# Ten gate/up pairs of a feed-forward layer: three of eight k steps by Strassen's seven products

## The chip, the cores and the metric

The kernel runs on one core of a Trainium2 chip. The metric is the device time of one execution in microseconds (us). TensorE is called PE here, its weight load PEld, VectorE DVE, ScalarE ACT, GpSimd POOL, and the queue that issues the weight transfers SP.

## The reference, cut

One layer of a decoder trunk on 256 tokens. The change touches the feed-forward part, the last four lines.

```python
h   = RMSNorm(x)                                   # x: (1, 256, 2048) float32
z   = h @ w_in                                     # one combined projection, 2048 x 19472
A   = GLA(h)                                       # chunked gated linear attention, 4 heads
Bm  = DilatedAttn(h)                               # 3 groups of 8 heads, joined by their denominators
y   = sigmoid(ga) * (A @ w_branch_gla) + sigmoid(gb) * (Bm @ w_branch_dil)
x   = x + y @ w_out
hf = _rmsnorm(x, ffn_norm[l])
gu = hf @ w_ffn_in[l]                              # 2048 x 11264
gate, up = gu[..., :D_FF], gu[..., D_FF:]          # D_FF = 5632
x = x + (jax.nn.silu(gate) * up) @ w_ffn_out[l]    # 5632 x 2048
out = _rmsnorm(x, final_norm)
```

## The kernel before

**Tiling.** All large products run over weights streamed once from HBM. A `Job` is one block of 512 output columns (or fewer) over `nkt` tiles of 128 rows (k tiles). Its weights come in units of four k tiles (1 MB, `dma`, line 172) into one of three `raw` buffers, and each unit is used in two subs of two k tiles, 128x1024 elements. `split` (line 184) makes two tiles of a sub: ACT copies it, rounded to fp32r, into `wh`, and DVE subtracts that from the raw tile into `wl`. There are five buffers of each (`LA` = 4 subs of lookahead). `mains` (line 241) then issues, for each k tile and each half of the tokens (128 rows), three matmuls into one PSUM bank: hi x wh, hi x wl and lo x wh, where hi and lo are the split activations, held stationary, and 512 weight columns move. A sub is 12 such matmuls, a gate or up job 8 subs or 96 matmuls, a gate/up pair 192.

**Order.** The program is written out in one order for all engines. For each sub the main loop emits, in this order: the split of the sub `LA` later, the evacuation of the job that ended just before (`pending.evac`), a hook of the job (`pre`), one step of a queue of small generators (`advance`), the matmuls of the sub, one more `advance`. Each engine works through its own part of this order; the tile framework puts in the waits.

**The feed-forward part.** Eleven pairs (`pair(p)`): a gate job, evacuated by two ACT instructions (Silu, `evac_fgate`), then an up job, evacuated by two DVE instructions (line 801, `evac_fup`). The product of 256 tokens x 512 columns is then turned by eight transposes into `psa` (`turn_block`, line 703) and split again by ACT and DVE (line 105). After pairs 4 and 8, and at the end, `down` multiplies the last four (at the end three) blocks by w_ffn_out in four jobs of 512 columns, each added into `x1` by DVE (line 810).

**PSUM** has eight banks of 128x512: four `acc`, one `psa` of two banks, two `psb`. A job in the feed-forward part takes two banks, `fpair` goes round acc, psb and acc.

**End.** The last job runs its token halves apart (lines 241 and 938), so that the final norm of the first half lies beside the matmuls of the second. In it, the sixth sub's split goes into `h` blocks.

Of the kernel before, what the change touches and what calls it, by code (L numbers as in the profile page):

```python
# [16 lines left out]
P = 128  # L17
D = 2048
S = 256
# [27 lines left out]
class Job:  # L47
# [2 lines left out]

    def __init__(self, kind, w, row0, nkt, col0, ncols, ktu, acts, evac, pre=None, pairs=None):
        self.pairs = pairs
        self.kind, self.w, self.row0, self.nkt = kind, w, row0, nkt
        self.col0, self.ncols, self.ktu = col0, ncols, ktu
        self.acts, self.evac, self.pre = acts, evac, pre or {}
# [3 lines left out]
def trunk_layer(ctx: ExitStack, tc: tile.TileContext, x, attn_norm, w_in, w_gk_up, b_gk, gla_norm,  # L61
# [18 lines left out]
    def ps_a():  # L80
        return psum.tile([P, 1024], F32, name="psa", tag="psa", bufs=1)
# [62 lines left out]
    epst = const.tile([P, 1], F32, name="epst")  # L144
    nc.vector.memset(epst, EPS)

    def add(job):
        jobs.append(job)
        job.subs = []
        job.units = []  # L150
        u1 = 0
# [12 lines left out]
        for i, s in enumerate(job.subs):  # L164
            s["last"] = i == len(job.subs) - 1

    def dma(unit):
        job = unit["job"]
        k, n = unit["k"], job.ncols
        unit["raw"] = ring.tile([P, 2048], F32, name="raw", tag="raw", bufs=NRAW)  # L170
        r0 = job.row0 + unit["k0"] * P
        nc.sync.dma_start(unit["raw"][:, :k * n].rearrange("p (a n) -> p a n", a=k),
                          job.w[r0:r0 + k * P, job.col0:job.col0 + n].rearrange("(a p) n -> p a n", p=P))

    def split(sub):
        n, k = sub["job"].ncols, sub["k"]
        src = sub["unit"]["raw"][:, sub["s0"] * n:(sub["s0"] + k) * n]
        if sub["job"] is jobs[-1] and sub["idx"] > LA:
            wh, wl = (block("h", 2 * (sub["idx"] - LA) + i, F32R) for i in range(2))
        else:  # L180
            wh = ring.tile([P, 1024], F32R, name="wh", tag="wh", bufs=LA + 1)
            wl = ring.tile([P, 1024], F32R, name="wl", tag="wl", bufs=LA + 1)
        act(wh[:, :k * n], src, AF.Copy)
        nc.vector.tensor_sub(wl[:, :k * n], src, wh[:, :k * n].bitcast(F32))  # L184
        sub["w"] = [t[:, :k * n].rearrange("p (a n) -> p a n", a=k) for t in (wh, wl)]

    def mains(sub, only=None, part=None):
        job = sub["job"]
        n = job.ncols
        wh, wl = sub["w"]  # L190
        if not hasattr(job, "acc"):
# [66 lines left out]
    def idle(n):  # L258

        for _ in range(2 * n + 1):  # L260
            yield
# [432 lines left out]
            act(z, z, AF.Sigmoid)  # L694
        return go

    def turn_block(src, hl):

        yield from idle(1)
        pt = ps_a()  # L700
        for j in range(4):
            for a in range(2):
                nc.tensor.transpose(pt[:, j * S + a * P:j * S + a * P + P], src[:, a, j * P:(j + 1) * P], ident)  # L703
        yield
        split_act(hl, pt.rearrange("p (j t) -> p j t", j=4))

    def evac_branch(key, i, last):
        def go(job):
# [42 lines left out]
    def reload_x():  # L751
        dctx.close()
        env["fp"] = ctx.enter_context(tc.tile_pool(name="ftmp", bufs=1))
        x1.extend(load_x("o", 4))
        for i in range(2):
            t = block("o", i)
            env["fg", i] = t
            nc.gpsimd.dma_start(t, bass.AP(tensor=final_norm.tensor, offset=final_norm.offset + i * 1024,
                                           ap=[[0, P], [1, 1024]]))

    def ffn_norm_chunk(c):
        yield from idle(1)
        hl = hl_block("h", 2 * c)
        x1T.append(hl)
        yield from to_blocks(x1[c], cols[:, 4 * c:4 * c + 4], hl, range(4),
                             quarters(ps_a()))
        if c == 3:
            tot = const.tile([P, 2], F32, name="tot1")
            nc.vector.tensor_reduce(tot, ss1, AX.X, ALU.add)
            env["rstd2"] = col_rstd("ffn", tot, D)  # L770

    def evac_out(c):
        def go(job):
            for a in range(2):
                nc.vector.tensor_add(x1[c][:, a], job.acc[a], x1[c][:, a])
                junk = env["fp"].tile([P, 512], F32, name="junk", tag="junk")
# [12 lines left out]
    def evac_fgate(p):  # L789
# [4 lines left out]
                act(z[:, a], job.acc[a], AF.Silu, scale=env["rstd2"][:, a:a + 1])  # L794
        return go

    def evac_fup(p):
        def go(job):
            z = env["sg"]
            for a in range(2):  # L800
                nc.vector.scalar_tensor_tensor(z[:, a], job.acc[a], env["rstd2"][:, a:a + 1], z[:, a],
                                               op0=ALU.mult, op1=ALU.mult)
            aT[p] = hl_block("z", (2 * p + 2) % 10)
            push("A", turn_block(z, aT[p]))
        return go

    def evac_down(c, last):
        def go(job):
            for a in range(2):
                nc.vector.tensor_add(x1[c][:, a], job.acc[a], x1[c][:, a])  # L810
                if last:
                    junk = env["fp"].tile([P, 512], F32, name="junk", tag="junk")
# [7 lines left out]
    def pair(p):  # L820
        for col, ev in ((512 * p, evac_fgate(p)), (FF + 512 * p, evac_fup(p))):
            first = (p, col) == (0, 0)
            add(Job("T", w_ffn_in, 0, KT, col, 512, 4, x1_acts, ev,
                    {5: lambda: drain("X")} if first else None, pairs=fpair()))

    def down(p0, n, last):
        acts = lambda ki, p0=p0: (aT[p0 + ki // 4], ki % 4)
        for c in range(4):
            pre = {2 * (n - 1): lambda: drain("A")} if c == 0 else None
            add(Job("T", w_ffn_out, p0 * 512, 4 * n, 512 * c, 512, 4, acts, evac_down(c, last), pre, pairs=fpair()))  # L830

# [84 lines left out]
    for i in range(done, len(subs) - len(jobs[-1].subs)):  # L916
        sub = subs[i]
        next_split()
        if i == 9:
            push("S", input_rstd())  # L920
        if pending and (pending is not jobs[0] or i >= 12):
            pending.evac(pending)
            pending = None
        hook = sub["job"].pre.get(sub["idx"])
        if hook:
            hook()
        advance()
        mains(sub)
        advance()
        if sub["last"]:  # L930
            pending = sub["job"]
# [4 lines left out]
    def add_tokens(src, a, q):  # L936
        w = slice(q * S, q * S + S)
        nc.vector.tensor_add(x1[3][:, a, w], src, x1[3][:, a, w])
        junk = env["fp"].tile([P, 512], F32, name="junk", tag="junk")
# [74 lines left out]
```

## Time and profile before

| | us |
|---|---|
| median of 3 runs | 1885.34 (1884.31 to 1885.46) |
| the profiled execution's own time | 1884.67 |
| its span, first to last instruction | 1882.9 |
| PE busy | 1868.8, 9324 instructions |
| DVE busy | 1025.3 |
| ACT busy | 861.2 |
| DMA engines, mean share of the span | some 5 tenths |

A matmul's recorded duration (386 ns in the mean) overlaps the next one's, so the pace of PE is read from a stretch divided by its count, not from the mean. DVE and ACT durations overlap their neighbours by less than 0.1 us. Between the span and the execution's own time lie 1.8 us.

### The profile page before, as it was taken

The numbers are of one execution on the slowest core, as the hardware profiler recorded it, in microseconds if no ns is written. First come the engines' busy times: TensorE is split into PE (matmuls) and PEld (weight loads), VectorE is DVE, ScalarE is ACT, GpSimd is POOL, SyncE is SP. The second block draws the span as 40 slices with busy tenths as digits, with TensorE's granted clock in tenths as the row PEclk, the third lists the DMA queues.
The fourth block names the chain that finished last, engine by engine and source line by source line (L and its number), as shares of the span: only waits on it lengthen the run. The fifth ranks groups of instructions, "written<-read, shape, count | busy, mean of one in ns | idle before, by whom it ended". The sixth has DMA issues, their size and how long they took to land.

```text
span 1882.9 us, 22862 instructions
## 1 busy us (share of the span) xinstructions
PE 1868.8 (99%) x9324; PEld 1589.8 (84%) x9324; DVE 1025.3 (54%) x1146; ACT 861.2 (46%) x1071; POOL 22.2 (1%) x35
## 2 busy tenths in 40 slices
PE   8999999999999999999999999999999999999998
PEld 8988988888888888888888888888888888888886
DVE  6446646745675466555554555444455454454454
ACT  6446545544454454544444455444443444434443
POOL 0000000000000000000000000000000000000001
PEclk9999999999999999999999999999999999999999
DMA  7554455456555565465657655555555555555553
GB/s 251 205 198 158 166 191 166 165 185 194 171 174 179 201 194 173 164 216 195 213 188 240 230 180 198 184 198 182 197 181 199 194 186 185 195 191 190 197 181 114
DMA packets 207299, 356.32 MB, mean 189 GB/s; under 512 B 6124, under 2 KB 66600, under 8 KB 207193
## 3 DMA queue, kind: packets, MB, share of 16 engines
q1 hardware_dynamic: 202192, 346.18, 54.2%
q0 software_dynamic: 1728, 5.51, 1.4%
q10 hardware_dynamic: 3272, 3.16, 0.6%
q8 instruction: 73, 1.20, 0.2%
q14 instruction: 34, 0.27, 0.0%
HBM read 352.70 MB, written 2.13 MB: 188 GB/s over the span
## 4 chain that ended last, share of the span: by engine, by line
PE 99%; DVE 0%; DMA 0%; ACT 0%; SPq 0%; issue 0%; DVEq 0%; ACTq 0%
PE acc L241 67%; PE psb L241 12%; PE acc L217 9%; PE acc L220 5%; PE psa L703 1%; PE psa L557 1%; PE psb L602 0%; PE psa L478 0%; PE psb L460 0%; PE psb L567 0%; PE psb L604 0%; PE psa L578 0%; DMA o<-in_x_dram 0%; PE psa L308 0%; PE psa L241 0%; PE psb L405 0%
## 5 line engine op out<-in xcount | busy, mean ns | idle before, releaser
L184 DVE TENSOR_TENSOR wl<-raw,wh 128x1024 fp32r<-128x1024 f32 (+2 forms) x655 | 794.3, 1216 | 784.6 <-ACT wh L121 783.1
L121 ACT ACTIVATE wh<-raw 128x1024 fp32r<-128x1024 f32 (+2 forms) x655 | 685.4, 1049 | 862.1 <-PE acc L241 642.2
L241 PE MATMUL acc<-wh,h 128*128 128x512 f32 (+2 forms) x2496 | 768.5, 386 | 0.0
L241 PEld LDWEIGHTS acc<-wh,h 128*128 128x128 f32 x2496 | 467.3, 188 | 91.3 <-issue 1.3
L241 PE MATMUL acc<-wl,h 128*128 128x512 f32 (+2 forms) x1248 | 480.0, 385 | 0.0
L241 PEld LDWEIGHTS acc<-wl,h 128*128 128x128 f32 x1248 | 235.1, 188 | 44.2 <-DVE wl L184 0.3
L241 PE MATMUL acc<-wh,z 128*128 128x512 f32 (+1 forms) x648 | 199.2, 386 | 0.0
L217 PE MATMUL acc<-h,wh 128*128 128x512 f32 x768 | 196.4, 397 | 0.0
L217 PEld LDWEIGHTS acc<-h,wh 128*128 128x128 f32 x768 | 138.5, 189 | 26.9 <-issue 0.7
L241 PEld LDWEIGHTS acc<-wh,z 128*128 128x128 f32 x648 | 121.1, 188 | 24.3
L241 PE MATMUL acc<-wl,z 128*128 128x512 f32 (+1 forms) x324 | 125.0, 386 | 0.0
L241 PE MATMUL psb<-wh,h 128*128 128x512 f32 x384 | 119.9, 390 | 0.0
L220 PEld LDWEIGHTS acc<-h,wl 128*128 128x128 f32 x768 | 104.6, 190 | 7.8
L220 PE MATMUL acc<-h,wl 128*128 128x256 f32 x768 | 106.9, 282 | 0.0
L241 PE MATMUL psb<-wh,z 128*128 128x512 f32 x304 | 94.9, 390 | 0.0
L241 PE MATMUL acc<-h,wh 128*128 128x256 f32 x512 | 92.5, 283 | 0.0
L241 PEld LDWEIGHTS psb<-wh,h 128*128 128x128 f32 x384 | 72.1, 188 | 14.9
L241 PEld LDWEIGHTS acc<-h,wh 128*128 128x128 f32 x512 | 80.0, 192 | 0.2
L241 PE MATMUL acc<-wh,o 128*128 128x512 f32 x256 | 79.5, 389 | 0.0
L241 PE MATMUL psb<-wl,h 128*128 128x512 f32 x192 | 74.7, 389 | 0.0
L241 PE MATMUL acc<-h,wl 128*128 128x256 f32 x256 | 72.4, 283 | 0.0
L241 PEld LDWEIGHTS acc<-wl,z 128*128 128x128 f32 x324 | 60.9, 188 | 12.1
(202 smaller groups left out, 1151.5 us busy)
## 6 DMA issues: line engine op xcount, KB each, us to landing
raw<-in_w_in_dram SPq DMA_DIRECT2D x144, 1024.0 KB, 4.7
raw<-in_w_ffn_in_dram SPq DMA_DIRECT2D x88, 1024.0 KB, 4.8
raw<-in_w_ffn_out_dram SPq DMA_DIRECT2D x44, 1024.0 KB, 5.0
raw<-in_w_branch_gla_dram SPq DMA_DIRECT2D x16, 1024.0 KB, 5.0
raw<-in_w_out_dram SPq DMA_DIRECT2D x16, 1024.0 KB, 5.0
raw<-in_w_branch_dil_dram SPq DMA_DIRECT2D x8, 1024.0 KB, 5.0
raw<-in_w_in_dram SPq DMA_DIRECT2D x8, 692.0 KB, 3.9
z<-in_b_gate_dram POOLq DMA_DIRECT2D x8, 512.0 KB, 8.0
```

What stands on the lines that cost most here:

```text
L121: nc.scalar.activation(o, i, func, **kw)
L184: nc.vector.tensor_sub(wl[:, :k * n], src, wh[:, :k * n].bitcast(F32))
L217: nc.tensor.matmul(job.acc[j], wh[:, kk, c], hl.both(aj), start=ki == 0, stop=ki == job.nkt - 1, skip_group_check=True)
L220: nc.tensor.matmul(job.acc[j][:, 0:S], wl[:, kk, c], hl.hi(aj), start=False, stop=ki == job.nkt - 1, skip_group_check=True)
L241: nc.tensor.matmul(dst, st, mv, start=first and i == 0 and j % per_bank == 0, stop=last and i == 2, skip_group_check=True)
L557: nc.tensor.matmul(p1[:, g * 256:(g + 1) * 256], qk[g][:, 0, 128:256], qk[g][:, 1], start=g != 1, stop=True, skip_group_check=True)
L703: nc.tensor.transpose(pt[:, j * S + a * P:j * S + a * P + P], src[:, a, j * P:(j + 1) * P], ident)
```

## The change

The product of two k tiles, both token halves and the gate and up columns is a 2x2 by 2x2 block product: A11, A12 (first token half, k tiles 0 and 1), A21, A22 (second half); B11, B12 (k tile 0, gate and up), B21, B22 (k tile 1). In pairs 1 to 10 gate and up become one job of kind "S" with eight steps of two k tiles. Five steps (0, 1, 3, 5, 7) are direct, with eight block products of three matmuls; three (`FAST` = 2, 4, 6) take seven, by Strassen's algorithm in Winograd's form, with sums of activation blocks (`x1_forms`, made once, used by all ten pairs) and sums of weight blocks (`sums`, made by DVE for each step). Pair 0 stays as it was.

- A direct step has two subs (b1, b2: one k tile, gate and up, 12 matmuls each). A Strassen step has four: b11 (512 wide, 3 matmuls), b2, t13 and t24 (1024 wide, 6 matmuls each). A job has 22 subs where a pair had 16.
- The 1 MB of a step (two k tiles, gate and up columns) comes in two transfers of 512 KB; before, the 1 MB of four k tiles of one job came in one.
- Eight PSUM banks are summed up in a job: p2, p3, p4, p8 by all steps, p1, p5, p6, p7 by the Strassen steps alone. The second four are read by `evac_step1` while step 7 runs, the first four by `evac_step2` after the job. `turn` says which four are in `acc`; it alternates between pairs that follow each other.
- From the first "S" job the lookahead is five subs, with one more buffer pair (blocks z8, z9) as every sixth.
- `turn_block` takes its banks from `ps_pair`, and is started one step of the queue later behind an "S" job. `down` follows pairs 3, 7 and 10; the last job's sixth split has a ring buffer; the final norm's weights are loaded into h6 and h7 when the last `down` begins.

The diff, cut: renamed scratch tags, unchanged lines and the constructor's rest are left out.

```diff
+    def __init__(self, kind, w, row0, nkt, col0, ncols, ktu, acts, evac, pre=None, pairs=None,
+                 col1=None, fast=(), forms=None, turn=0):
         self.pairs = pairs
+        self.col1, self.fast, self.forms = col1, fast, forms
+        self.bank, self.turn = {}, turn
...
+    def add_steps(job):
+
+        seen = {}
+        for st in range(job.nkt // 2):
+            unit = dict(job=job, k0=2 * st, k=2, raw=None)
+            units.append(unit)
+            if st in job.fast:
+                plan = (("b11", ((0, "a11", "p1"),)), ("b2", ((0, "a12", "p2"), (1, "s4", "p3"))),
+                        ("t13", ((0, "s1", "p5"), (1, "s3", "p7"))), ("t24", ((0, "s2", "p6"), (1, "a22", "p4"))))
+            else:
+                plan = tuple((f"b{a + 1}", ((0, f"a1{a + 1}", "p2"), (1, f"a1{a + 1}", "p3"),
+                                            (0, f"a2{a + 1}", "p4"), (1, f"a2{a + 1}", "p8"))) for a in range(2))
+            for src, prods in plan:
+                sub = dict(job=job, unit=unit, step=st, src=src, idx=len(job.subs), prods=[])
+                for f, a, b in prods:
+                    pr = dict(f=f, a=a, b=b, first=b not in seen, last=False)
+                    seen[b] = pr
+                    sub["prods"].append(pr)
+                job.subs.append(sub)
+                subs.append(sub)
+        for pr in seen.values():
+            pr["last"] = True
+        for i, s in enumerate(job.subs):
+            s["last"] = i == len(job.subs) - 1
+
...
+    def sums(sub):
+
+        if sub.get("src") not in ("t13", "t24"):
+            return
+        b = raw_step(sub["unit"])
+        if sub["src"] == "t13":
+            t = sub["unit"]["t"] = env["fp"].tile([P, 4, 512], F32, name="t", tag="t")
+            nc.vector.tensor_sub(t[:, 0:2], b[:, :, 1], b[:, 0])
+        else:
+            t = sub["unit"]["t"]
+            nc.vector.tensor_sub(t[:, 2], b[:, 1, 1], t[:, 0])
+            nc.vector.tensor_sub(t[:, 3], b[:, 1, 0], t[:, 2])
...
+    def step_src(sub):
+        b = raw_step(sub["unit"])
+        src = sub["src"]
+        if src == "b11":
+            return b[:, 0, 0:1]
+        if src[0] == "b":
+            return b[:, int(src[1]) - 1]
+        return sub["unit"]["t"][:, 0:2] if src == "t13" else sub["unit"]["t"][:, 2:4]
...
+    def step_bank(job, b):
+
+        if (b in ("p2", "p3", "p4", "p8")) == (job.turn == 0):
+            job.bank[b] = ps_acc()
+        else:
+            for names, i in ((("p2", "p3"), 2), (("p4", "p8"), 3), (("p7", "p6"), 2), (("p1", "p5"), 3)):
+                if b in names:
+                    job.bank.update(zip(names, ps_pair(i)))
+
+    def step_mains(sub):
+        job = sub["job"]
+        for pr in sub["prods"]:
+            if pr["b"] not in job.bank:
+                step_bank(job, pr["b"])
+            wh, wl = (t[:, pr["f"]] for t in sub["w"])
+            hi, lo = step_acts(job, sub["step"], pr["a"])
+            for i, (st, mv) in enumerate(((hi, wh), (hi, wl), (lo, wh))):
+                nc.tensor.matmul(job.bank[pr["b"]], st, mv, start=pr["first"] and i == 0,
+                                 stop=pr["last"] and i == 2, skip_group_check=True)
...
+        if job.kind == "S":
+            for a in range(2):
+                w = job.w[r0 + a * P:r0 + a * P + P]
+                nc.sync.dma_start(raw_step(unit)[:, a],
+                                  bass.AP(tensor=w.tensor, offset=w.offset + job.col0,
+                                          ap=[list(w.ap[0]), [job.col1 - job.col0, 2], [1, n]]))
+            return
...
+    def ring_pair(sub):
+
+        if sub["extra"]:
+            return [block("z", 8 + i, F32R) for i in range(2)]
+        return [ring.tile([P, 1024], F32R, name=m, tag=m, bufs=LA + 1) for m in ("wh", "wl")]
+
     def split(sub):
+        if sub["job"].kind == "S":
+            src = step_src(sub)
+            n = src.shape[1]
+            wh, wl = (t[:, :n * 512].rearrange("p (a n) -> p a n", a=n) for t in ring_pair(sub))
+            act(wh, src, AF.Copy)
+            nc.vector.tensor_sub(wl, src, wh.bitcast(F32))
+            sub["w"] = [wh, wl]
+            return
...
-        if sub["job"] is jobs[-1] and sub["idx"] > LA:
-            wh, wl = (block("h", 2 * (sub["idx"] - LA) + i, F32R) for i in range(2))
-        else:
-            wh = ring.tile([P, 1024], F32R, name="wh", tag="wh", bufs=LA + 1)
-            wl = ring.tile([P, 1024], F32R, name="wl", tag="wl", bufs=LA + 1)
+        wh, wl = ring_pair(sub)
...
-    def turn_block(src, hl):
-
-        yield from idle(1)
-        pt = ps_a()
+    def turn_block(src, hl, n=1, pair=2):
+
+        yield from idle(n)
+        pt = ps_pair(pair)
         for j in range(4):
             for a in range(2):
-                nc.tensor.transpose(pt[:, j * S + a * P:j * S + a * P + P], src[:, a, j * P:(j + 1) * P], ident)
-        yield
-        split_act(hl, pt.rearrange("p (j t) -> p j t", j=4))
+                nc.tensor.transpose(pt[j // 2][:, (j % 2) * S + a * P:(j % 2) * S + a * P + P],
+                                    src[:, a, j * P:(j + 1) * P], ident)
+        yield
+        for i in range(2):
+            act(hl.t[i][:, :, 0], pt[i].rearrange("p (j t) -> p j t", j=2), AF.Copy)
+        for i in range(2):
+            nc.vector.tensor_sub(hl.t[i][:, :, 1], pt[i].rearrange("p (j t) -> p j t", j=2),
+                                 hl.t[i][:, :, 0].bitcast(F32))
...
+    def load_fg():
         for i in range(2):
-            t = block("o", i)
+            t = block("h", 6 + i)
             env["fg", i] = t
             nc.gpsimd.dma_start(t, bass.AP(tensor=final_norm.tensor, offset=final_norm.offset + i * 1024,
                                            ap=[[0, P], [1, 1024]]))
...
+    FAST = (2, 4, 6)
+    x1F = {}
+
+    def x1_forms():
+
+        yield from idle(1)
+        for n, st in enumerate(FAST):
+            t = x1T[st // 2].t[st % 2]
+            a = env["fp"].tile([P, 2, S], F32, name="fa", tag="u0")
+            f = env["fp"].tile([P, 4, P], F32, name="ff", tag="u1")
+            nc.vector.tensor_add(a, t[:, :, 0].bitcast(F32), t[:, :, 1].bitcast(F32))
+            nc.vector.tensor_add(f[:, 0], a[:, 0, P:], a[:, 1, P:])
+            nc.vector.tensor_sub(f[:, 2], a[:, 0, 0:P], a[:, 0, P:])
+            nc.vector.tensor_sub(f[:, 1], f[:, 0], a[:, 0, 0:P])
+            nc.vector.tensor_sub(f[:, 3], a[:, 1, 0:P], f[:, 1])
+            b = x1F[st] = block("o", n, F32R).rearrange("p (w f q) -> p w f q", w=2, f=4)
+            act(b[:, 0], f, AF.Copy)
+            nc.vector.tensor_sub(b[:, 1], f, b[:, 0].bitcast(F32))
+            yield
+            yield
...
+            push("F", x1_forms())
...
+    def turn_up(p, z, n, pair):
+        aT[p] = hl_block("z", 2 * p % 8)
+        push("A", turn_block(z, aT[p], n, pair))
...
-            aT[p] = hl_block("z", (2 * p + 2) % 10)
-            push("A", turn_block(z, aT[p]))
+            turn_up(p, z, 1, 2)
...
+    def evac_step1(job):
+
+        u = job.u = [env["fp"].tile([P, 512], F32, name=f"u{i}", tag=f"u{i}") for i in range(4)]
+        b = job.bank
+        act(u[0], b["p1"], AF.Copy)
+        nc.vector.tensor_add(u[1], u[0], b["p6"])
+        nc.vector.tensor_add(u[2], u[1], b["p7"])
+        nc.vector.tensor_add(u[1], u[1], b["p5"])
+        nc.vector.tensor_add(u[3], u[2], b["p5"])
+
+    def evac_step2(p):
+        def go(job):
+            u, b = job.u, job.bank
+            z = env["fp"].tile([P, 2, 512], F32, name="sg", tag="sg", bufs=2)
+            nc.vector.tensor_add(z[:, 0], u[0], b["p2"])
+            act(z[:, 0], z[:, 0], AF.Silu, scale=env["rstd2"][:, 0:1])
+            nc.vector.tensor_add(u[1], u[1], b["p3"])
+            nc.vector.tensor_add(z[:, 1], u[2], b["p4"])
+            act(z[:, 1], z[:, 1], AF.Silu, scale=env["rstd2"][:, 1:2])
+            nc.vector.tensor_add(u[3], u[3], b["p8"])
+            for a in range(2):
+                nc.vector.scalar_tensor_tensor(z[:, a], u[1 + 2 * a], env["rstd2"][:, a:a + 1], z[:, a],
+                                               op0=ALU.mult, op1=ALU.mult)
+            turn_up(p, z, 2, 2 * job.turn)
         return go
...
             add(Job("T", w_ffn_in, 0, KT, col, 512, 4, x1_acts, ev,
-                    {5: lambda: drain("X")} if first else None, pairs=fpair()))
+                    {5: lambda: drain("X")} if first else None, pairs=[3] if col >= FF else [0]))
+
+    def fast_pair(p, turn):
+        def start():
+            drain("F")
+            drain("A")
+        job = Job("S", w_ffn_in, 0, KT, 512 * p, 512, 2, x1_acts, evac_step2(p), {4: start}, None,
+                  FF + 512 * p, FAST, lambda st: x1F[st], turn)
+        add(job)
+        job.pre[len(job.subs) - 2] = lambda: evac_step1(job)
...
             pre = {2 * (n - 1): lambda: drain("A")} if c == 0 else None
-            add(Job("T", w_ffn_out, p0 * 512, 4 * n, 512 * c, 512, 4, acts, evac_down(c, last), pre, pairs=fpair()))
-
-    for p in range(11):
-        pair(p)
-        if p == 4:
-            down(0, 4, False)
-        if p == 8:
-            down(4, 4, False)
+            if c == 0 and last:
+                pre[0] = load_fg
+            add(Job("T", w_ffn_out, p0 * 512, 4 * n, 512 * c, 512, 4, acts, evac_down(c, last), pre,
+                    pairs=[((3, 0, 1, 3), (0, 1, 0, 3))[p0 == 4][c]]))
+
+    pair(0)
+    for p in range(1, 11):
+        fast_pair(p, (0, 0, 1, 0, 0, 1, 0, 1, 0, 1, 0)[p])
+        if p in (3, 7):
...
+    more = next(i for i, s in enumerate(subs) if s["job"].kind == "S") + LA + 1
+    for i, s in enumerate(subs):
+        s["extra"] = i >= more and (i - more) % (LA + 2) == 0
...
+            if i + 1 < len(subs):
+                sums(subs[i + 1])
...
+        if i + LA + 1 == more:
+            next_split()
```

## Rows read from the trace of the kernel before

**Rows 1.** The page's heads: span, busy time and share by engine, chain that ended last.

```profile
span 1882.9 us, 22862 instructions
PE 1868.8 (99%) x9324; PEld 1589.8 (84%) x9324; DVE 1025.3 (54%) x1146; ACT 861.2 (46%) x1071; POOL 22.2 (1%) x35
...
PE 99%; DVE 0%; DMA 0%; ACT 0%; SPq 0%; issue 0%; DVEq 0%; ACTq 0%
```

**Rows 2.** Waits of PE, whole span: total us, times, longest.

```profile
PE psb L843 <- DMA grow<-in_attn_norm_dram: 3.6, 1, 3.6
PE psb L308 <- DMA o<-in_x_dram: 1.4, 1, 1.4
PE acc L241 <- DVE h L184: 0.4, 1, 0.4
```

**Rows 3.** Chain in order of time, feed-forward pair: start us, us, what.

```profile
1283.02 0.87 PE psa L703 x8
1283.89 16.34 PE acc L241 x72
1300.23 21.76 PE psb L241 x96
1321.99 5.44 PE acc L241 x24
```

**Rows 4.** Windows, one pair: busy us of each engine, PEclk, DMA share, GB/s.

```profile
1283.89:1328.30 44.41, 44.41 (x201) 36.87 (x201) 22.14 (x20) 19.10 (x21) 0.00 (x0) 1.00 0.55 189
```

**Rows 5.** Groups by shape, DVE: busy us, mean ns, idle before.

```profile
L184 DVE TENSOR_TENSOR wl<-raw,wh 128x1024 fp32r<-128x1024 f32 x631 | 773.4, 1229 | 773.9 <-ACT wh L121 772.4
...
L801 DVE SCALAR_TENSOR_TENSOR sg<-acc,r_ffn,sg 128x512 f32<-128x512 f32 x16 | 11.2, 744 | 0.0
...
L713 DVE TENSOR_TENSOR z<-z,z 128x512 f32<-128x512 f32 x8 | 5.5, 693 | 0.3
```

**Rows 6.** Timeline of DVE, a branch's evacuation: start us, us, instruction, idle before.

```profile
823.68 1.23 DVE L184 TENSOR_TENSOR wl<-raw,wh 128x1024 fp32r<-128x1024 f32 x1 [1.49 <-ACT wh L121]
824.82 0.68 DVE L711 TENSOR_TENSOR z<-acc,z 128x512 f32<-128x512 f32 x1
825.54 0.69 DVE L713 TENSOR_TENSOR z<-z,z 128x512 f32<-128x512 f32 x1
826.14 0.69 DVE L711 TENSOR_TENSOR z<-acc,z 128x512 f32<-128x512 f32 x1
```

**Rows 7.** Timeline around the change from a gate to an up job.

```profile
1299.84 0.39 PE L241 MATMUL acc<-wh,h 128*128 128x512 f32 x1
...
1300.26 1.06 ACT L121 ACTIVATE wh<-raw 128x1024 fp32r<-128x1024 f32 x1 [1.66 <-PE acc L241]
...
1301.36 1.23 DVE L184 TENSOR_TENSOR wl<-raw,wh 128x1024 fp32r<-128x1024 f32 x1 [1.49 <-ACT wh L121]
```

**Rows 8.** Groups by shape, ACT: busy us, mean ns, idle before.

```profile
L121 ACT ACTIVATE z<-psa 128x512 fp32r<-128x512 f32 x30 | 16.0, 587 | 0.0
...
L121 ACT ACTIVATE junk<-o 128x512 f32<-128x512 f32 x18 | 11.4, 633 | 13.5 <-DVE o L775 7.6 <-DVE o L810 5.7
L121 ACT ACTIVATE sg<-acc,r_ffn 128x512 f32<-128x512 f32 x16 | 10.0, 674 | 0.0
```

**Rows 9.** DMA issues by line: count, KB each, median us to landing.

```profile
raw<-in_w_ffn_in_dram SPq DMA_DIRECT2D x88, 1024.0 KB, 4.8
...
o<-in_x_dram SPq DMA_DIRECT2D x4, 512.0 KB, 8.1
```

**Rows 10.** Timeline at the end: POOL and DVE, then PE's wait.

```profile
1860.60 2.54 POOL L815 TENSOR_TENSOR o<-o,o 128x512 f32<-128x512 f32 x2 [13.76 <-ACT junk L121]
...
1862.27 1.96 DVE L184 TENSOR_TENSOR h<-raw,h 128x1024 fp32r<-128x1024 f32 x1 [1.90 <-ACT h L121]
...
1864.28 1.43 PE L241 MATMUL acc<-h,z 128*128 128x512 f32 x5 [0.45 <-DVE h L184]
```

More of the change, by code (lines that the diff above doesn't have):

```diff
@@ L47 @@
 class Job:
-    def __init__(self, kind, w, row0, nkt, col0, ncols, ktu, acts, evac, pre=None, pairs=None):
+    def __init__(self, kind, w, row0, nkt, col0, ncols, ktu, acts, evac, pre=None, pairs=None,
+                 col1=None, fast=(), forms=None, turn=0):
         self.pairs = pairs
+        self.col1, self.fast, self.forms = col1, fast, forms
+        self.bank, self.turn = {}, turn
         self.kind, self.w, self.row0, self.nkt = kind, w, row0, nkt
@@ new lines, in raw_step @@
+    def raw_step(unit):
+        return unit["raw"].rearrange("p (a c n) -> p a c n", a=2, c=2)
+    def sums(sub):
[9 more added lines that the diff above has]
+            nc.vector.tensor_sub(t[:, 3], b[:, 1, 0], t[:, 2])
@@ new lines, in step_src, with step_acts @@
+    def step_src(sub):
[6 more added lines that the diff above has]
+        return sub["unit"]["t"][:, 0:2] if src == "t13" else sub["unit"]["t"][:, 2:4]
+    def step_acts(job, st, a):
+        if a[0] == "s":
+            f = job.forms(st)
+            return [f[:, w, int(a[1]) - 1] for w in range(2)]
+        hl, j = job.acts(2 * st + int(a[2]) - 1)
+        q = slice(0, P) if a[1] == "1" else slice(P, 2 * P)
+        return hl.hi(j)[:, q], hl.lo(j)[:, q]
@@ L150, in add @@
         job.units = []
+        if job.kind == "S":
+            add_steps(job)
+            return
         u1 = 0
@@ L171, in dma @@
         r0 = job.row0 + unit["k0"] * P
+        if job.kind == "S":
+            for a in range(2):
[4 more added lines that the diff above has]
+            return
         nc.sync.dma_start(unit["raw"][:, :k * n].rearrange("p (a n) -> p a n", a=k),
                           job.w[r0:r0 + k * P, job.col0:job.col0 + n].rearrange("(a p) n -> p a n", p=P))
+    def ring_pair(sub):
+        if sub["extra"]:
+            return [block("z", 8 + i, F32R) for i in range(2)]
+        return [ring.tile([P, 1024], F32R, name=m, tag=m, bufs=LA + 1) for m in ("wh", "wl")]
     def split(sub):
+        if sub["job"].kind == "S":
[5 more added lines that the diff above has]
+            sub["w"] = [wh, wl]
+            return
         n, k = sub["job"].ncols, sub["k"]
         src = sub["unit"]["raw"][:, sub["s0"] * n:(sub["s0"] + k) * n]
-        if sub["job"] is jobs[-1] and sub["idx"] > LA:
-            wh, wl = (block("h", 2 * (sub["idx"] - LA) + i, F32R) for i in range(2))
-        else:
-            wh = ring.tile([P, 1024], F32R, name="wh", tag="wh", bufs=LA + 1)
-            wl = ring.tile([P, 1024], F32R, name="wl", tag="wl", bufs=LA + 1)
+        wh, wl = ring_pair(sub)
         act(wh[:, :k * n], src, AF.Copy)
@@ L188, in mains @@
         job = sub["job"]
+        if job.kind == "S":
+            step_mains(sub)
+            return
         n = job.ncols
@@ L775, in go @@
                 nc.vector.tensor_add(x1[c][:, a], job.acc[a], x1[c][:, a])
-                junk = env["fp"].tile([P, 512], F32, name="junk", tag="junk")
+                junk = env["fp"].tile([P, 512], F32, name="junk", tag="u3")
                 act(junk, x1[c][:, a], AF.Square, accum_out=ss1[:, a, c:c + 1])
@@ L802, in go @@
                                                op0=ALU.mult, op1=ALU.mult)
-            aT[p] = hl_block("z", (2 * p + 2) % 10)
-            push("A", turn_block(z, aT[p]))
+            turn_up(p, z, 1, 2)
+        return go
+    def evac_step1(job):
[20 more added lines that the diff above has]
+            turn_up(p, z, 2, 2 * job.turn)
         return go
@@ L811, in go @@
                 if last:
-                    junk = env["fp"].tile([P, 512], F32, name="junk", tag="junk")
+                    junk = env["fp"].tile([P, 512], F32, name="junk", tag="u3")
                     act(junk, x1[c][:, a], AF.Square, accum_out=ss2[:, a, c:c + 1])
@@ L829, in down @@
             pre = {2 * (n - 1): lambda: drain("A")} if c == 0 else None
-            add(Job("T", w_ffn_out, p0 * 512, 4 * n, 512 * c, 512, 4, acts, evac_down(c, last), pre, pairs=fpair()))
-    for p in range(11):
-        pair(p)
-        if p == 4:
-            down(0, 4, False)
-        if p == 8:
-            down(4, 4, False)
+            if c == 0 and last:
[6 more added lines that the diff above has]
+        if p in (3, 7):
+            down(p - 3, 4, False)
     down(8, 3, True)
@@ L938, in add_tokens @@
         nc.vector.tensor_add(x1[3][:, a, w], src, x1[3][:, a, w])
-        junk = env["fp"].tile([P, 512], F32, name="junk", tag="junk")
+        junk = env["fp"].tile([P, 512], F32, name="junk", tag="u3")
         act(junk[:, 0:S], x1[3][:, a, w], AF.Square, accum_out=ss2[:, a, 3 + q:4 + q])
```

## The prediction

> **What bounds the kernel now.** I read the page's heads and the chain first: PE is busy 99% of the span, and the chain that ended last is PE for 99% of it [rows 1]. The waits say the same from the other side: after the prologue PE waits once, 0.4 us, near the end [rows 2]. So in the feed-forward part time is matmuls times their pace, and nothing else. The pace comes from the chain in order of time: 96 matmuls in 21.76 us, 0.2267 us each, the same in 72 and 24 of them, and the eight transposes of a pair take 0.87 us [rows 3]. A direct pair is 192 x 0.2267 + 0.87 = 44.4 us, as its window shows; in it DVE is busy 22.1 and ACT 19.1 us, at full clock [rows 4]. The other question is therefore how much room DVE and ACT have beside PE, for the change pays for matmuls with their work.
>
> **What it removes.** A Strassen step has 21 matmuls for 24. Three steps in each of ten pairs: 30 x 3 = 90 matmuls x 0.2267 = 20.4 us. The transposes stay. A fast pair is then 183 x 0.2267 + 0.87 = 42.36 us of PE.
>
> **What DVE gets.** Its back-to-back pace is read from starts: 1.14 us from a 1024-wide subtraction to the next instruction, 0.60 us for a 512-wide one whose successor doesn't need its result, 0.72 where it does [rows 6]; the last form with two operands and a scalar is taken at 0.70, its duration [rows 5] less the same overlap. In a fast pair: 1024-wide, 10 splits of direct steps, 3 x 3 of Strassen steps and 3 sums, 22 x 1.14 = 25.1; 512-wide, 3 splits (b11), 6 sums, 4 + 4 additions of the two evacuations and 2 of the turn, 19 x 0.60 plus 5 x 0.12 for dependent ones = 12.0; two scalings 1.4. Together 43 instructions and 38.5 us beside PE's 42.36. Nothing in the trace shows a sum of two strided blocks of a raw tile; the bounds are the pace above and the full recorded durations without any overlap (1.23, 0.69, 0.74 [rows 5]): 22 x 1.23 + 19 x 0.69 + 2 x 0.74 = 41.7. Both lie under 42.36. I take 38.5, as rows 6 show one DVE instruction starting 0.09 us ahead of its predecessor's recorded end.
>
> [...]
>
> **What ACT gets.** 19 rounded copies of 1024 at 1.06, 3 of 512 and one out of PSUM at some 0.6, two Silu at 0.67, two copies of the turn at 0.59 [rows 7, 8]: 20.1 + 2.5 + 1.3 + 1.2 = 25.1 us of 42.36. It has room, but it stands in one queue, so its waits count.
>
> **Does it fit in time?** An average doesn't say. I walked one pair, with 0 where PE starts it, by this rule: with six buffers the copy of sub s may start when PE has ended sub s-6, 0.03 us after its last matmul; it takes 1.06 and DVE follows 0.04 later [rows 7]. PE's own times are then 0, 2.72, 5.44, transposes at 8.16, 9.03, 11.75 (first Strassen step), 16.51, 21.95 (second), 26.71, 32.15 (third), 36.91, 39.63, end 42.35.
> - Head: DVE sums for t13 and splits b2 by 2.5, then the evacuation of the pair before (six instructions with two Silu between) by 6.2. PE wants the result for the transposes at 8.16: 2.0 us of room. ACT's next copy waits behind the second Silu until 5.0; t13's halves are done at 8.6 and t24's at 9.7, wanted at 13.8 and 15.2.
> - Middle: t13 and t24 of the second step are done at 19.5 and 20.6, wanted at 24.0 and 25.4; of the third at 29.7 and 30.8, wanted at 34.2 and 35.6. DVE falls behind in each Strassen step and waits again in each direct one (at 22 and at 32).
> - Foot: the first evacuation stands in DVE's queue behind the split of the next pair's fourth sub. The copies start 0.05 after 32.15, 34.19, 35.55 and 36.91 at the earliest, so that split ends at 39.2, and the four additions at 41.8. The next pair puts its first sums into these banks: the first at 42.35 into those read by 40.6, the second at 43.0 into one read by 41.8. That leaves 1.2 to 1.7 us, the narrowest place, ten times.
> With the full durations the foot moves by some 0.7 us and still fits. So PE doesn't stall, by the walk.
>
> **Transfers and what is only moved.** A raw buffer is free when DVE has read it, and its next step is split some 10 us later but for the first Strassen step of the next pair: freed at 34.5, first wanted at 39.9, 5.4 us for a landing of 4.8 [rows 9]. For halves of 512 KB the trace has only the four loads of x, issued together, 8.1 us [rows 9]. At that bound the copy of b11 slips by 2.7 us, and with it the queue into the next head; the product is wanted at 54.1, and of the head's 2.0 us about 1.4 would go. So 0, and at the bound still about 0. On SP nothing else is queued in these pairs.
>
> [...]
>
> The activation sums are 18 short DVE instructions and three copies, at most 18 x 0.69 = 12.4 us, in pair 0, where DVE has 22 us free [rows 4]: 0. The moved load of the norm's weights is issued by POOL when pair 10 ends and is wanted 16 us later: 0. The turn ahead of the last `down` comes 2.7 us later than before and is wanted by its fifth sub at 11.8; by the walk its first half is split at 11.1: 0, at most 1 us once. At the end PE's wait of 0.45 us goes: it was for a split that took 1.96 us with POOL beside it [rows 10], and that split now comes before that work.
>
> **Sum.** Profiled execution 1884.67 - 20.4 - 0.45 = 1863.8; the median of the runs lies 0.67 above that execution: 1864.5.
>
> **Rivals.**
> 1. *A late hand-over of the banks, or DVE just short.* PE would wait at the head of each fast pair, 0.3 to 0.9 us in ten of them: 1867 to 1873.5. For it: the 1.2 us of room at the foot, and DVE at 91 to 98% of PE. Against: even the full durations fit. It shows as PE waiting on DVE, at an addition of the first evacuation or a weight tile wl.
> 2. *DVE becomes the bound and the kernel slower.* Place: all ten fast pairs. The pair is DVE's where its 38.5 exceeds 42.36, 0.09 us more per instruction on 43; the gain is gone at 42.36 + 2.04 = 44.4, 0.14 us more per instruction. One thing in the trace makes a DVE instruction so much longer: a split beside a POOL multiplication, 1.96 instead of 1.23 [rows 10]. Were all 22 wide ones like that, a pair would be 38.5 + 22 x 0.73 = 54.6 and the kernel 1864.5 + 10 x 12.2 = 1987. Against: POOL computes nothing in these pairs (0.00 in the window [rows 4]); what else would lengthen DVE's instructions, PE and ACT and DMA running beside them, already runs beside the rows I used. With half of that effect, 46.6 and 1906.
> 3. *The matmuls go but the time doesn't*: stalls at the heads, the transposes and the transfers together take 1.7 to 2.5 us of each pair's 2.04. 1881.6 to 1889.1. For it only that three places are within 2 us.
> 4. *PE's pace changes with shorter subs.* Subs of 3 and 6 matmuls have more waits per matmul; between subs, banks, and jobs of 12 no gap shows at 0.2267 [rows 3], so this is put into the width: 0.005 us on 1830 matmuls is 9 us, counted with the first rival.
>
> **How the numbers follow.** No stall: 0.70, 1862.5 to 1867. First rival with the fourth: 0.17, to 1873.5. Third: 0.06. Second: 0.07. The range holds the first two, 1862.5 to 1873.5. About 0.2%, 3.8 us, is what a measurement of this kernel can tell from no change; faster 0.87, same 0.06, slower 0.07.
>
> **What would show it.** Right: PE's chain in the fast pairs at 42.4 us from pair to pair, 9234 matmuls and transposes on PE, no wait of PE longer than 0.3 us there, DVE busy some 40 us of a pair, and DVE's waits for wh near the second and third direct step. Wrong in the price of DVE: instructions longer than 1.23 and 0.69, or starts further apart than 1.14 and 0.60. Wrong in the order: a row of PE waiting for an addition at a pair's head, for the scaling before the transposes, or for wl in a Strassen step. Wrong in PE: 96 matmuls in other than 21.8 us.

## The result and the profile after

The changed kernel takes 1864.13 us (median; 1863.59 to 1864.82) where the kernel before takes 1885.31 in the same runs: a ratio of 0.9889, 95% interval 0.9872 to 0.9906. 21.2 us are gone; the forecast was 1864.5 and 20.85.

The page's heads after, against [rows 1] (span; busy us, share and instructions of each engine; the chain's shares):

```profile
span 1861.5 us, 23268 instructions
PE 1847.5 (99%) x9234; PEld 1572.2 (84%) x9234; DVE 1197.6 (64%) x1394; ACT 913.2 (49%) x1144; POOL 22.3 (1%) x35
...
PE 99%; DMA 0%; DVE 0%; ACT 0%; SPq 0%; issue 0%; DVEq 0%; ACTq 0%
```

90 instructions fewer on PE, 172 us more work on DVE, 52 more on ACT, and the chain is PE's as before. All waits of PE after (total us, times, longest), against [rows 2]:

```profile
PE psb L1027 <- DMA grow<-in_attn_norm_dram: 3.8, 1, 3.8
PE psb L423 <- DMA o<-in_x_dram: 1.5, 1, 1.5
```

Both lie in the prologue; the wait at the end, 0.4 us [rows 2, 10], is gone. One fast pair (pair 5), in the same columns as [rows 4]:

```profile
1445.00:1487.37 42.37, 42.37 (x192) 35.17 (x192) 38.76 (x44) 24.19 (x27) 0.00 (x0) 1.00 0.57 202
```

PE needs 42.37 us where a direct pair took 44.41, and DVE fills 38.76 of them. The foot of that pair on DVE (timeline: start us, us, instruction):

```profile
1484.21 0.68 DVE L959 TENSOR_TENSOR u<-u,acc 128x512 f32<-128x512 f32 x1
1484.93 0.69 DVE L960 TENSOR_TENSOR u<-u,acc 128x512 f32<-128x512 f32 x1
1485.65 0.69 DVE L961 TENSOR_TENSOR u<-u,acc 128x512 f32<-128x512 f32 x1
1486.25 0.68 DVE L962 TENSOR_TENSOR u<-u,acc 128x512 f32<-128x512 f32 x1
1486.85 0.69 DVE L289 TENSOR_TENSOR wl<-raw,wh 128x512 fp32r<-128x512 f32 x1
```

These are the four additions of the first evacuation. Counted from the pair's start at 1445.00, the second ends at 40.6 and the fourth at 41.9, and the pair at 42.37: what the walk gave (40.6, 41.8, 42.35). The next pair's first matmul starts at 1487.21 (the chain counts a pair from 0.16 us later), so the second addition, which ends at 1485.62, is 1.6 us ahead of it; the walk said 1.75. Starts are 0.72 apart where an addition needs the result of the one before it, or overwrites what that one reads (the third), and 0.60 elsewhere. The transfers landed as follows (count, KB each, median us), against [rows 9]:

```profile
raw<-in_w_ffn_in_dram SPq DMA_DIRECT2D x160, 512.0 KB, 4.4
...
raw<-in_w_ffn_in_dram SPq DMA_DIRECT2D x8, 1024.0 KB, 4.7
```

### The profile page after: what moved, and what is told of

The parts are those of the page before. It is cut to its first block, busy times and chain, and to the rows that moved or that the text cites. A ratio compares the mean times of both kernels' runs of the same rounds, so it can differ in the third digit from the quotient of the medians.

```text
span 1861.5 us, 23268 instructions
## 1 busy us (share of the span) xinstructions
PE 1847.5 (99%) x9234; PEld 1572.2 (84%) x9234; DVE 1197.6 (64%) x1394; ACT 913.2 (49%) x1144; POOL 22.3 (1%) x35
## 3 DMA queue, kind: packets, MB, share of 16 engines
q8 instruction: 72, 1.18, 0.2%
## 4 chain that ended last, share of the span: by engine, by line
PE 99%; DMA 0%; DVE 0%; ACT 0%; SPq 0%; issue 0%; DVEq 0%; ACTq 0%
PE acc L356 51%; PE acc L236 12%; PE acc L332 10%; PE psb L356 6%; PE psa L236 5%; PE acc L335 5%; PE psb L236 5%; PE psa L672 1%; PE psb L717 0%; PE psa L593 0%; PE psa L818 0%; PE psb L575 0%; PE psb L682 0%; PE psb L719 0%; PE acc L818 0%; PE psa L693 0%
## 5 line engine op out<-in xcount | busy, mean ns | idle before, releaser
L133 ACT ACTIVATE wh<-raw 128x1024 fp32r<-128x1024 f32 (+3 forms) x614 | 625.8, 1026 | 633.6 <-PE acc L356 435.6
L296 DVE TENSOR_TENSOR wl<-raw,wh 128x1024 fp32r<-128x1024 f32 (+2 forms) x482 | 580.9, 1212 | 505.7 <-ACT wh L133 503.8
L356 PE MATMUL acc<-wh,h 128*128 128x512 f32 (+2 forms) x1536 | 469.8, 383 | 0.0
L356 PEld LDWEIGHTS acc<-wh,h 128*128 128x128 f32 x1536 | 286.6, 188 | 54.2 <-issue 1.3
L356 PE MATMUL acc<-wl,h 128*128 128x512 f32 (+2 forms) x768 | 292.9, 381 | 0.0
L356 PE MATMUL acc<-wh,z 128*128 128x512 f32 x600 | 187.8, 390 | 0.0
L289 DVE TENSOR_TENSOR wl<-raw,wh 128x1024 fp32r<-128x1024 f32 (+1 forms) x132 | 143.1, 1100 | 42.3 <-ACT wh L133 41.9
L356 PEld LDWEIGHTS acc<-wl,h 128*128 128x128 f32 x768 | 144.7, 188 | 25.5
L236 PE MATMUL acc<-wh,h 128*128 128x512 f32 x446 | 146.7, 390 | 0.0
L356 PE MATMUL acc<-wl,z 128*128 128x512 f32 x300 | 116.7, 389 | 0.0
L236 PEld LDWEIGHTS acc<-wh,h 128*128 128x128 f32 x446 | 83.7, 188 | 17.3
```

What stands on the lines that cost most here:

```text
L133: nc.scalar.activation(o, i, func, **kw)
L236: nc.tensor.matmul(job.bank[pr["b"]], st, mv, start=pr["first"] and i == 0, stop=pr["last"] and i == 2, skip_group_check=True)
L289: nc.vector.tensor_sub(wl, src, wh.bitcast(F32))
L356: nc.tensor.matmul(dst, st, mv, start=first and i == 0 and j % per_bank == 0, stop=last and i == 2, skip_group_check=True)
```

## Experiments

**Is it the matmuls alone?** The first kernel keeps all of the rearrangement and makes every step direct:

```diff
-    FAST = (2, 4, 6)
+    FAST = ()
...
-        job.pre[len(job.subs) - 2] = lambda: evac_step1(job)
```

with the two evacuations replaced by the Silu and scaling of a direct pair.

> The changed kernel with no Strassen step: the ten pairs keep their joint jobs of eight steps, the alternating banks, the sixth buffer, the halves of 512 KB and the new order, but all steps are direct (192 matmuls a pair). Theory (the time is matmuls times 0.2267 us, the rest of the change costs and gives nothing but the 0.45 us at the end): 1864.1 + 90 x 0.2267 = 1884.5 us. Rival (a part of the gain comes from the new order, the lookahead or the banks): clearly under 1884, say 1875 to 1882. DVE falls back to some 22 us of a 44.4 us pair.

Measured: 1884.69 us, 0.9998 (0.9988 to 1.0007) of the kernel before. The second has one step, `FAST = (4,)`.

> One Strassen step in each of the ten pairs (step 4) in place of three. Theory (price per matmul): 30 matmuls less than all direct, 1884.5 - 6.8 = 1877.7 us. If the first evacuation of p1, p5, p6, p7 or the hand-over of banks cost something each pair whatever the number of steps, the time lies above the line through the all-direct kernel and the one with three steps, by that cost times ten.

Measured: 1877.61 us. From no step to one are 7.1 us, from one to three 13.5 us, 6.7 a step; the price by the rows was 6.8. The traces say it pair by pair: the transposes behind pairs 4 and 5 start as follows with no, one and three steps.

```profile
1461.61 1.03 PE L818 MATMUL acc<-ident,sg 128*128 128x128 f32 x8
1506.02 1.03 PE L818 MATMUL psa<-ident,sg 128*128 128x128 f32 x8
...
1459.76 1.03 PE L818 MATMUL acc<-ident,sg 128*128 128x128 f32 x8
1503.49 1.03 PE L818 MATMUL psa<-ident,sg 128*128 128x128 f32 x8
...
1453.00 1.03 PE L818 MATMUL acc<-ident,sg 128*128 128x128 f32 x8
1495.37 1.03 PE L818 MATMUL psa<-ident,sg 128*128 128x128 f32 x8
```

A pair takes 44.41, 43.73 and 42.37 us: 0.68 for each step, and 44.41 as before without one. The rearrangement gives nothing that can be measured, and there is no cost a pair that would not depend on the number of steps. This is shown.

**When does DVE become the bound?** Four steps, `FAST = (2, 3, 4, 6)`.

> Four Strassen steps in each pair (2, 3, 4 and 6). PE's work falls by 30 matmuls more, to 41.68 us a pair. If PE were the bound still: 1864.1 - 6.8 = 1857.3 us. DVE by its pace of starts: 24 x 1.14 + 22 x 0.60 + 6 x 0.12 + 1.4 = 42.7 us a pair, so that DVE becomes the bound and the gain is eaten: 1864 to 1868 us, with PE waiting for wl or for an addition by about 1 us a pair. By the full recorded durations without overlap DVE has 24 x 1.23 + 22 x 0.69 + 2 x 0.74 = 46.2 us a pair: about 1900 us.

Measured: 1869.34 us, 5.2 more than with three steps, though PE has 6.8 us less to do, and 1.3 above the range that the sum by starts gave. One stretch, from the wait in one pair to the wait at the same place in the next (columns as in [rows 4]), and PE's timeline there, in the next pair's third Strassen step:

```profile
1471.22:1514.40 43.18, 42.32 (x188) 34.48 (x188) 42.68 (x48) 25.09 (x30) 0.00 (x0) 1.00 0.57 195
```

```profile
1511.27 0.39 PE L236 MATMUL psb<-wh,h 128*128 128x512 f32 x1
1511.49 0.39 PE L236 MATMUL acc<-wh,h 128*128 128x512 f32 x1
1511.94 0.50 PE L236 MATMUL acc<-wl,h 128*128 128x512 f32 x1
...
1513.20 0.40 PE L236 MATMUL psb<-wh,o 128*128 128x512 f32 x1
1514.40 0.50 PE L236 MATMUL psb<-wl,o 128*128 128x512 f32 x1 [0.80 <-DVE wl L289]
```

DVE is busy 42.68 of 43.18 us; by the starts of [rows 6] it had 42.7, by full durations it would have had 46.2. So the sum by starts is the right one, and with four steps DVE is the bound, 42.7 us of its work beside 41.7 of PE's. The timeline teaches a second thing: the gap from 1511.49 to 1511.94 is twice the usual 0.227 and has no wait beside it, and the row of 0.80 stands for a gap of 1.20. A matmul is recorded 0.39 us long while the next may start after 0.227, so a wait shows 0.16 us short, and a short one (0.22 us here, 0.30 in a later experiment) doesn't show at all. The waits of this kernel add up to 6.6 us; its periods from one pair's transposes to the next pair's are together 12.3 us longer than PE's work, and 12.0 is what separates 1869.3 from the 1857.3 of a kernel that PE bounds.

**Do the bank roles matter?** All pairs with `turn` 0, the turned block always through psa, and the second `down` in the order of banks of the others:

```diff
-            turn_up(p, z, 2, 2 * job.turn)
+            turn_up(p, z, 2, 2)
...
-                    pairs=[((3, 0, 1, 3), (0, 1, 0, 3))[p0 == 4][c]]))
+                    pairs=[(3, 0, 1, 3)[c]]))
...
-        fast_pair(p, (0, 0, 1, 0, 0, 1, 0, 1, 0, 1, 0)[p])
+        fast_pair(p, 0)
```

> The bank roles no longer alternate: p2, p3, p4, p8 of every pair lie in acc, and the turned block always goes through psa. Theory (the alternation is what hides the second evacuation): the first sums of the next pair go into banks that the second evacuation still reads; in the changed kernel its first addition ends 3.0 us after the pair before, so PE waits some 3 us at each of the seven places where a fast pair follows a fast pair: 1864.1 + 21 to 22 = 1885 to 1886 us. Rival (the hand-over of banks is no matter): 1864 us.

Measured: 1897.29 us, 1.0065 (1.0050 to 1.0080) of the kernel before: slower than without Strassen at all. PE's waits (total us, times, longest), and two of the seven places with the granted clock behind them (windows, columns as in [rows 4], the clock third from the end):

```profile
PE acc L236 <- DVE sg L968: 22.2, 7, 3.2
```

```profile
1235.17:1243.54 8.37, 8.37 (x24) 6.63 (x25) 5.49 (x8) 2.40 (x3) 0.00 (x0) 0.64 0.32 98
1283.81:1292.26 8.45, 8.45 (x38) 6.95 (x39) 6.63 (x9) 3.46 (x4) 0.00 (x0) 1.00 0.29 99
```

The seven waits are the expected ones: 3.18 us each on the second evacuation's first addition. They make 22.2 of 33.2 us. The rest is the clock: behind five of the seven waits the granted clock was below 1.00 in the next 8.4 us (0.64 in the mean at one, 0.79 to 0.80 at four; 1.00 at the other two). In the first of them matmuls start 0.427 us apart, where 0.227 is the pace elsewhere:

```profile
1236.16 1.06 PE L236 MATMUL acc<-wh,h 128*128 128x512 f32 x2
1237.01 0.63 PE L236 MATMUL acc<-wl,h 128*128 128x512 f32 x1
1237.44 1.05 PE L236 MATMUL acc<-wh,h 128*128 128x512 f32 x2
```

By an estimate from these means, a loss of 1 - mean of each stretch, PE lost 8.4 x 0.36 = 3.0 us at the first and 8.4 x 0.2 = 1.7 at each of the four: 9.8 us. The count agrees: the first has 24 matmuls in 8.37 us, 2.9 more than 24 x 0.2267. With seven times the hidden 0.16 that is 33.1 of 33.2. The periods from transposes to transposes agree: against the changed kernel's they are 3.4 to 3.5 us longer at the two hand-overs without a fall of the clock, 5.0 to 5.1 at four and 6.3 at the first, 33.4 in all. I had priced waits at face value.

**How much room is at the foot?** The first evacuation one sub later:

```diff
-        job.pre[len(job.subs) - 2] = lambda: evac_step1(job)
+        job.pre[len(job.subs) - 1] = lambda: evac_step1(job)
```

> The first evacuation is emitted one sub later, before the pair's last sub, and so stands in DVE's queue behind one split more. By the changed kernel's rows it then ends 1.7 us later: where the next job starts in acc (after pairs 2, 5, 7 and 9) its second sum finds a bank read 0.6 us too late, elsewhere the first finds its banks free at about the time it wants them. Theory (the foot has 1.1 to 1.75 us of room): PE waits 0.6 us four times and 0 to 0.1 us six times, 1866 to 1867.5 us. Rival (the foot has more room than that): 1864 us and no wait. Second rival (the room is used up already): each of ten places 1.7 us later, 1881 us.

Measured: 1871.67 us, 7.5 more than the changed kernel, and neither the size nor the places that I expected. PE's waits that have a row, and DVE ahead of the longest:

```profile
PE psb L356 <- DVE u L962: 4.1, 2, 2.4
...
PE psb L356 <- ACT u L133: 0.2, 1, 0.2
```

```profile
1789.46 1.23 DVE L296 TENSOR_TENSOR wl<-raw,wh 128x1024 fp32r<-128x1024 f32 x1 [2.78 <-ACT wh L133]
1790.61 0.68 DVE L959 TENSOR_TENSOR u<-u,psa 128x512 f32<-128x512 f32 x1
```

They lie where `down` follows, behind pairs 3 (1.65 us) and 10 (2.45 us). There the split that now stands ahead of the additions is 1024 wide, not b11's 512, and behind pair 10 its copy waited 2.9 us for a transfer of w_ffn_out: DVE stood still for 2.78 us with the additions queued behind. After the 2.45 us the clock fell once more, to 0.67 in the mean from 1793.38 to 1798.00. Between fast pairs no wait has a row, but one of 0.3 us is there, at the start of pair 2 for one (the second addition on DVE, then PE's last matmul of pair 1 and first of pair 2):

```profile
1229.99 0.69 DVE L960 TENSOR_TENSOR u<-u,psa 128x512 f32<-128x512 f32 x1
...
1230.30 0.39 PE L236 MATMUL acc<-wh,h 128*128 128x512 f32 x1
1230.82 0.47 PE L236 MATMUL psa<-wh,h 128*128 128x512 f32 x1
```

Matmuls that start 0.227 apart elsewhere start 0.52 apart here, the second 0.14 us behind the end of the addition that reads psa. The same gap stands at the start of pairs 5, 7 and 9, so after pairs 1, 4, 6 and 8, where the next pair begins in psa, and each of the four periods from transposes to transposes is 0.42 us longer than the changed kernel's. I had expected 0 to 0.1 us there, and 0.6 where the next job begins in acc, after pairs 2, 5, 7 and 9. In acc there is no gap. Behind pair 2 the addition that should have been 0.6 us late ended at 1274.79, while pair 3's second product had started at 1274.00. So that product doesn't lie in p5's bank, and the order in which the banks of acc are handed on was misread. Four times 0.42, 2.0 us behind pair 3 and 4.8 behind pair 10 (the wait, what its row leaves out, and the clock) make 8.5 us, where the span of this trace is 8.3 longer. Where the next pair begins in psa, the foot of the changed kernel thus has some 1.4 us of room: the evacuation came 1.7 later, and PE 0.3. In acc it has more than the 1.2 us of the walk. The trace puts the wait behind pair 10 down to the transfer; the same late landing (2.6 us, on ACT) is in the changed kernel too, hidden by the lookahead.

**Is the sixth buffer what carries the Strassen steps?** Without it, and with a lead of four subs:

```diff
-        s["extra"] = i >= more and (i - more) % (LA + 2) == 0
+        s["extra"] = s["job"] is jobs[-1] and s["idx"] > LA
...
-        if i + LA + 1 == more:
-            next_split()
```

> The lookahead stays at four subs with five buffer pairs, as in the kernel before; only the last job's sixth split has the extra blocks. Theory (what is late in a Strassen step is DVE's work, not the buffers): the splits of t13 and t24 still end some 3.5 us ahead of PE, so no wait in the pairs; only the split at the end is late again, 0.45 us: 1864.6 us. Rival (the sixth buffer carries the Strassen steps): PE waits in each of thirty steps, up to one sub of 1.36 us: 1870 to 1905 us.

Measured: 1865.12 us, and one wait beyond the prologue, at the end:

```profile
PE psb L356 <- DVE z L296: 0.5, 1, 0.5
```

As expected: the buffers aren't the limit with three steps, and the wait of 0.45 us at the end belongs to the later split, which takes 1.97 us, as it took 1.96 beside POOL before [rows 10]. Its price is more than its row: the matmuls before and behind it start 0.84 us apart in place of 0.23.

**The rival that makes it slower.** The sums `t` on POOL, `nc.gpsimd` for `nc.vector` in `sums`.

> The sums of weight blocks (t) are made by POOL in place of DVE. DVE's own work falls by 3 x 2.46 to 31.1 us a pair. Theory (the rival by which the kernel becomes slower, tried on purpose): POOL takes 1.27 us for 512 columns, 15.3 us a pair, and a DVE instruction beside it loses 0.73 us of 0.87 us, as at the end of the kernel before; DVE is then worth 31.1 + 12.9 = 44.0 us a pair, more than PE's 42.37: about 1880 us, with DVE instructions well above 1.23 us. Without any such effect POOL's sums are hidden and nothing changes: 1864 us with DVE at 31 us.

Measured: 1864.38 us, unchanged. But DVE isn't relieved. The window of pair 5 (POOL before the clock), and DVE's groups in it (count, busy us, mean ns):

```profile
1445.00:1487.37 42.37, 42.37 (x193) 35.17 (x192) 38.60 (x35) 24.43 (x27) 19.52 (x10) 1.00 0.59 198
```

```profile
L289 DVE TENSOR_TENSOR wl<-raw,wh 128x1024 fp32r<-128x1024 f32 x9 | 13.5, 1512 | 3.4 <-ACT wh L133 3.2
...
L289 DVE TENSOR_TENSOR wl<-raw,wh 128x512 fp32r<-128x512 f32 x3 | 4.9, 1624 | 0.0
...
L968 DVE TENSOR_TENSOR sg<-u,acc 128x512 f32<-128x512 f32 x1 | 0.7, 675 | 0.0
```

Nine instructions left DVE and its busy time fell from 38.76 to 38.60: the splits of raw tiles grew from 1222 to 1512 ns and from 684 to 1624, instructions that read PSUM kept their 0.68, and the splits of the sums, beside which POOL stands idle here, took 1211 ns. The lengthening of [rows 10] is there again. Its price was too high: 19.5 us of POOL lengthened DVE's work by 7.5 (38.60 less the 31.1 expected without the sums), 0.38 us a microsecond, not 0.84. That a part of POOL's time lay beside reads of PSUM or pauses explains only some of this: by the timelines nearly 15 us a pair lay beside splits of raw tiles, which lost about half a microsecond for each, and unevenly (one took 3.22 us, another, beside POOL for 1.18 us, no more than 1.23). What decides which split loses is not shown.

**Is there something left to gain?** Four steps only in pairs 1, 4 and 8, which start without arrears on DVE:

```diff
-    FAST = (2, 4, 6)
+    FAST = (2, 3, 4, 6)
...
-                  FF + 512 * p, FAST, lambda st: x1F[st], turn)
+                  FF + 512 * p, FAST if p in (1, 4, 8) else (2, 4, 6), lambda st: x1F[st], turn)
```

> Four Strassen steps (2, 3, 4, 6) in pairs 1, 4 and 8 alone, which follow a direct pair or a down, three (2, 4, 6) in the other seven. With four in all ten, PE waited in the seven pairs that follow a fast pair and in the two jobs behind pairs 3 and 10, and not in pairs 1, 4 and 8. Theory (DVE starts these three pairs without arrears, and the pair behind them, with three steps, has 3.6 us of DVE time over to take up what is left): no wait, 3 x 3 x 0.2267 = 2.0 us less than with three steps everywhere: 1862.1 us. Rival (the arrears come through at the hand-over to pairs 2, 5 and 9, where the first evacuation has 1.1 to 1.75 us of room): 1864 us or more.

Measured: 1862.86 us, 0.9884 (0.9869 to 0.9899) of the kernel before in the same runs, which is no measurable difference from the changed kernel's 0.9889. In the trace the fourth step gives half of its 0.68 us: from the turn of pair 0 to that of pair 7 are 385.70 us, against 386.37, with two of the three pairs in between (1195.39 to 1581.09, 1193.91 to 1580.28). Most of the rest is lost at the start of pairs 2, 5 and 9, behind each of them, where the first matmul starts 0.34 to 0.41 us after the one before it, without a row of waiting. At pair 5 (the second addition, then PE):

```profile
1444.68 0.69 DVE L960 TENSOR_TENSOR u<-u,psa 128x512 f32<-128x512 f32 x1
...
1445.11 0.39 PE L236 MATMUL acc<-wh,h 128*128 128x512 f32 x1
1445.52 0.47 PE L236 MATMUL psa<-wh,h 128*128 128x512 f32 x1
```

So the rival had the place right, the first evacuation at the hand-over, and the theory's "no wait" was wrong; the arrears take half of the gain, not all of it. And four steps everywhere, with only step 2's sums on POOL, at the time when DVE reads PSUM:

> Four Strassen steps in all ten pairs, and the weight sums of step 2 alone are made by POOL, at the time at which DVE reads PSUM for the second evacuation (those DVE instructions stayed at 0.68 us beside POOL in the run with all sums on POOL; the splits out of SBUF were lengthened, b11 from 0.69 to 1.31 and b2 from 1.22 to 1.89 us). DVE: 42.7 - 2.46 + 1.3 = 41.5 us a pair beside PE's 41.68. Theory (the place of POOL's work decides): the bound goes back to PE but for small waits, 1857.5 to 1861 us. Rival (POOL takes back whatever it takes over, as when all sums were on it): 1869 us.

Measured: 1866.28 us (1864.15 to 1866.89); the trace is of the execution that took 1864.15. Between the two: two of its pairs take 41.8 and 41.9 us from turn to turn, against 42.37 with three steps, and a third 42.2, with DVE busy for 41.82; but the turns of pairs 0 and 2 and the two jobs behind pairs 3 and 10 wait. No version tried beats the changed kernel by more than the measurement can tell.

## Why the prediction was right

- *The bound and the price of a matmul.* 90 x 0.2267 us: the three kernels with no, one and three steps lie on that line to within 0.4 us, and their pairs in the traces to within 0.01.
- *DVE's sum.* 38.5 forecast, 38.76 busy. That starts and not durations are the right price for these queued instructions is settled by the kernel with four steps, where 42.7 was forecast and 42.68 came. By full durations a pair of that kernel would have held 46.2 us of DVE work; the 43.18 us that one took don't agree with it.
- *The walk.* Head: the product was ready at 6.1 us (6.2 forecast), wanted at 8.2. Foot: 40.6 and 41.9. DVE waited for wh three times in a pair, for 3.1 us in all, in direct steps. Two things were read wrongly: which bank of acc the second product gets, where the room was larger than said, and the room before pairs that begin in psa, some 1.4 us and not 1.75. The sum didn't depend on either.
- *Transfers.* The halves landed in 4.4 us, well inside the bound of 8.1. The share of the DMA engines went from 0.55 to 0.57, and in the kernel with the halves and no Strassen step a pair took 44.41 us, as before: to give up the transfers of 1 MB cost nothing here.
- *The end.* The cause was right: the wait returns when the split is late again. The term was too small, since it took the wait at its row. From pair 0's transposes to the end the traces differ by 21.1 us, of which 20.4 are matmuls; the other 0.7 lie behind the last pair. That the median came out within 0.4 us is partly luck: pair 0's transposes, ahead of all that the experiments change, start anywhere from 1193.6 to 1195.2 us in these traces, the last experiment's left aside.
- *The rivals' prices.* The first, and the third with it, priced a wait of PE at its length. Where waits of 3.2 us were made, they cost half as much again: seven such hand-overs cost 33 us, not 22, with the granted clock at 0.64 to 0.80 in the mean behind five of them. What the second rival feared was there (1222 ns became 1512 with the sums on POOL), but its price per instruction was taken from one split, 0.87 us of which lay beside POOL, and was twice too high for a stretch (0.84 us a microsecond of POOL, where 0.38 came). The fourth had no price to pay: a pair with shorter subs takes the 42.37 us that 0.2267 a matmul gives.

## What to carry to other kernels

Here arithmetic could be traded from PE, the bound, to the half idle DVE [rows 1], as the walk through one period, at the pace of starts, left room at every hand-over; the average alone (38.8 of 42.4 us with three steps, 42.7 of 41.7 with four) allowed three steps and not four. Who reads which PSUM bank last is part of the change: with the same matmuls, a fixed assignment of banks turned a gain of 21 us into a loss of 12.

## What the runs showed of the hardware

- With the fixed banks PE stood still for 3.18 us at seven places; in the next 8.1 to 8.5 us its granted clock was 0.64 in the mean at one, 0.79 to 0.80 at four and 1.00 at two. After the one wait of 2.45 us, with the evacuation later, it was 0.67 over 4.6 us; behind the wait of 1.65 us there, and behind those of 0.8 us with four steps, 1.00. What decides between the seven isn't settled.
- In these streams of 512 columns a wait of PE was recorded some 0.16 us short (a row of 0.80 for a gap of 1.20 at a pace of 0.227), and waits of 0.22 and 0.30 us had no row: a matmul was recorded 0.39 us long.
- POOL's sums beside a busy DVE took 2.79 us in the mean for 1024 columns and 1.87 to 2.09 for 512, where POOL's multiplication of 512 took 1.29 in the same run.
